# Small transposes as products with the identity, and a scaling moved from GpSimd's keys to VectorE's products, in a chunked recurrence

## The chip, the cores and the metric

The kernel runs on one core of a Trainium2 chip. The metric is the device time of one execution in microseconds (us): 3152.22 us, the median of three runs (3151.61 to 3154.9). Engine names in the profile: PE is TensorE, PEld its weight loads, DVE is VectorE, ACT is ScalarE, POOL is GpSimd, SP is the queue that issues the DMAs. Matrix products here are in float32; PE's clock has two levels, 1.2 and 2.4 GHz, which the profile shows as a granted share of 0.50 and 1.00.

## The reference

Three blocks over 512 latent tokens and 256 context tokens of 1024 channels: two transformer layers, and a third block that mixes a gated short convolution with a recurrence of eight heads, followed by a mixture of 16 experts. The change lies in that recurrence, which runs once forwards and once backwards over the tokens. Per head, with a state S of 64 values x 64 keys:

```python
def step(s, inp):
    r_t, w_t, k_t, v_t, a_t, b_t = inp
    sa = jnp.einsum('bhvk,bhk->bhv', s, a_t)
    s = s * w_t[:, :, None, :] + sa[..., :, None] * b_t[:, :, None, :] + v_t[..., :, None] * k_t[:, :, None, :]
```

The context gives the state in which the latents start.

## The kernel before, in words

The recurrence is computed in chunks of 64 tokens. Both directions are worked on at once: rows 0 to 63 of every tile belong to the forward direction (d = 0), rows 64 to 127 to the backward one (d = 1). `rwkv_prep` builds the operands of all chunks, `rwkv_scan` then walks from chunk to chunk. `rwkv_prep` runs three times, and these are the three stretches of which the prediction speaks:

- the context's, 8 heads and 4 chunks, beside the last feed-forward products of the second layer (lines 430, 432, 435), at about 1860 to 2040 us of the span;
- the first four latent heads', 8 chunks, beside the projections of the third block (the same lines), about 2100 to 2330 us;
- the other four latent heads', beside an output projection (line 2258) and the normalising of the first heads (lines 1174, 1187, 2201, 2215), about 2400 to 2560 us.

Within one `rwkv_prep`, after the elementwise work:

1. `products` (line 1909) multiplies keys and queries; VectorE masks the results into `M1`.
2. `tri_inverse` inverts triangular 64 x 64 blocks: VectorE runs 62 small operations, each of which needs the one before, and then 32 x 32 transposes (lines 2014, 2029, 2037, 2038). Their result feeds PE's 32 x 32 products (lines 2045, 2055).
3. `value_part` runs beside it. For each chunk: a product (1909), ScalarE takes it out of PSUM, GpSimd masks it (`M2`), PE multiplies it with the values (lines 1957, 1967). Then `by_time(kts)` turns the keys: GpSimd scales each head's keys by `pc0`, the decay over the whole chunk, in place (lines 1924 to 1926); PE transposes 64 x 64 blocks, one for each chunk, head and direction, with `flip` (lines 1771 and 1773); 16 of them fill a PSUM bank, which ScalarE empties. Then `kv`: products of the turned keys and the values (line 1981), one bank for each chunk, emptied by ScalarE (line 1983). Then `by_time(bts)` does the same turning for the second set of keys.

`flip` has two forms. The block that goes to rows 0 to 63 of PSUM is a transpose instruction (line 1771), the one that goes to rows 64 to 127 a product with the identity (line 1773). The loop in `by_time` takes d = 0 and d = 1 in turn, so the two forms alternate on PE.

A float32 product is two records in the trace (two weight loads and two matmuls), a transpose one.

`pcs` holds the same decays as `pc0`, but the backward half is ordered by step and not by chunk, as `kv` is; GpSimd copies them (lines 1895, 1897) before the products of step 1.

Generators (`braid`, `weave`) mix a stretch's parts at given rates, and each engine's list of instructions is fixed when the program is built; an engine takes its list strictly in order. PSUM has eight banks of 512 columns, divided between the parts: five for the latents' `rwkv_prep`, three for what runs beside it (in the second latent stretch), and a part waits when all its banks are full. Most elementwise instructions are issued by helpers and carry the helper's line: 382 (`act`, ScalarE), 385 (`tt`, tensor_tensor on VectorE or GpSimd), 388 (`stt`).

Of the kernel before, what the change touches and what calls it, by code (L numbers as in the profile page):

```python
# [167 lines left out]
def _run(g):  # L168
    """a generator to its end -> what it returns"""
    try:  # L170
        while True:
            next(g)
    except StopIteration as e:
        return e.value


def _parts(t):
    """two ranges of tokens"""
    return [(0, TL), (TL, TA)] if t == TA else [(0, TC), (TC, TL)]


class _Hook:
    """a generator step by step; what it returns"""
# [19 lines left out]
class _Arena:  # L203
    """SBUF, float32 left of a movable bound and float32r right of it, each side a stack of tiles.
    Long-lived buffers lie at the outer ends, transient ones rotate near the bound.
    Zones set memory aside for work that other work is to overlap."""
# [37 lines left out]
    def move(self, mid, *cuts):  # L244
        """float32 up to mid floats, float32r behind; new tiles end at the cuts"""
# [18 lines left out]
    def reserve(self, z, n, dt=F32, below=SIZE):  # L264
        """set n floats aside for zone z"""
# [48 lines left out]
    def forget(self, n):  # L314
        """the order of the last releases alone counts from here on"""
# [45 lines left out]
class _K:  # L361
# [50 lines left out]
    def prefetch(self, key, src):  # L412
        """split weights ahead of their use"""
        self.pre[key] = self.wsplit(src, top=True)
# [10 lines left out]
    def gemm(self, w, nk, acts, outs):  # L425
        """outs: list of (psum AP, token slice); w: function (hi|lo, k) -> lhsT; acts: list of (hi, lo) per k"""
# [22 lines left out]
    def rstd_cols(self, cols, n, scale, eps, op=OP.add):  # L449
        """1 / sqrt(cols * scale <op> eps), with a Newton step behind the square root's table"""  # L450
# [11 lines left out]
    def rms_bcast(self, acc, t, nfeat):  # L462
        """acc [128, t]: sums of squares per partition; -> bank with 1/rms on every partition"""
# [9 lines left out]
    def col_bcast(self, r, n):  # L473
        """[128, n] -> bank with the n * 128 values along each partition"""
# [6 lines left out]
    def sumsq(self, blocks, t, w=None, bufs=None, pool=None):  # L481
        """sum over blocks of squares, [128, t]; with w a second one, of the blocks times columns of w"""
# [21 lines left out]
    def modulate(self, xs, t, pb, segs, us=None, dve=()):  # L504
        """xs: list of f32 [128, t]; segs: list of (slice, scale fn(k), shift fn(k)); us: two APs for the normed values or
        None; -> list of (hi, lo) Bufs"""
# [17 lines left out]
    def norm_parts(self, xs, t, nfeat, segs, pool=0, low=((), ())):  # L524
        """normed and modulated blocks, range of tokens by range -> list of (hi, lo) Bufs"""
# [12 lines left out]
    def modulate_part(self, outs, xs, t0, t1, r, segs, low=()):  # L538
        """low: the blocks whose low part is left to GpSimd"""
# [22 lines left out]
    # log1p(e) for 0 <= e <= 1, elementwise on small tiles  # L562
# [31 lines left out]
    def ada(self, parts, w=2):  # L594
        """parameters of layer 0 -> Buf [128, 48, 2]: block-major vectors, (latent, context); params 1 and 4 are 1 + scale"""
# [30 lines left out]
    def ada_first(self, h):  # L626
        """half h of the blocks of layer 0's first shift and scale"""
# [15 lines left out]
        # block 8 j + 4 h + n at column (n, j, v)  # L643
# [8 lines left out]
    def ada_rows(self):  # L652
        """the same for layers 1 and 2 (context: shift and scale 0 alone), as VectorE's sums of products along the rows of
        the transposed weights"""
# [37 lines left out]
    # ---------------------------------------------------------------- layer 0  # L692
# [49 lines left out]
    def gated(self, x, p, P, gate, n, t0, t1, two):  # L742
        """x += gate * p over a range of tokens"""
# [5 lines left out]
    def out_proj(self, w, y, T, x, P, gate, k0=0, name=None, hook=None):  # L749
        """x += gate * (rows k0... of w)^T y; with a hook range of tokens by range, and the hook behind each"""  # L750
# [28 lines left out]
    def step(self, g, n, z=1):  # L779
        """n steps of work in a zone"""  # L780
# [8 lines left out]
    def ffn(self, l, P, T, x, a, side, rate, start=0, hook=None):  # L789
        """x += gate * swiglu(a); a: normed blocks as (hi, lo) Bufs; the last sums range of tokens by range, with a hook  # L790
        behind each"""
# [5 lines left out]
        def outs(bg, bu, bc, t0, t1):  # L797
            """gate's and up's PSUM over a range of tokens"""
# [27 lines left out]
        for g, nb in enumerate(FFG):  # L826
            j0 = 0
            last = g == len(FFG) - 1
            if g == 0:
                # the first two blocks range by range: the second range's norm is under way  # L830
# [55 lines left out]
    def mixer0(self, ab, P):  # L886
# [7 lines left out]
        # dt, [16, tokens]  # L894
# [1846 lines left out]
```

## Time and profile before

| | |
|---|---|
| median of the runs | 3152.22 us |
| profiled execution, first to last instruction (span) | 3154.1 us |
| PE busy | 2976.9 us, 94% |
| DVE busy | 1702.1 us, 54% |
| ACT busy | 989.3 us, 31% |
| POOL busy | 312.5 us, 10% |
| mean granted clock of PE | 0.947 |
| share of PE in the chain that ended last | 71% |
| of it, line 1773 and line 1771 | 2% and 1% of the span |

The profile gives no other time of the profiled execution than its span; it lies inside the range of the three runs. Busy shares are means over stages with different limits, so the stretches are read one by one. "Idle before, releaser" is the time for which an engine stood still before an instruction, and whose work ended that wait. Matmuls are pipelined: a record's duration is longer than the distance to the next record's start, and it is the distance that PE's time is made of.

### The profile page before, as it was taken

What the parts mean: (1) busy time and instruction counts of PE and PEld (TensorE: products, weight loads), DVE (VectorE), ACT (ScalarE), POOL (GpSimd) and SP (SyncE); (2) the same over time, 40 slices, a digit from 0 to 9 for tenths busy, and PEclk for the clock granted to TensorE, in tenths of its full rate; (3) what the DMA queues carried; (4) which work ended last, traced back from release to release, by engine and by line L of the source; (5) the groups of instructions that cost most, each with busy time, mean ns of one, the idle gap of its engine ahead of it and who ended that gap; (6) DMA issues with size and microseconds to landing.
All of it is one profiled execution on the core that took longest, in us unless ns stands there. A gap on an engine that the chain in (4) does not pass through costs nothing.

```text
span 3154.1 us, 43364 instructions
## 1 busy us (share of the span) xinstructions
PE 2976.9 (94%) x17688; PEld 2113.3 (67%) x17688; DVE 1702.1 (54%) x2713; ACT 989.3 (31%) x1625; POOL 312.5 (10%) x287
## 2 busy tenths in 40 slices
PE   7999999999999989999999999988899998999997
PEld 4776558888888877554788777775675565344443
DVE  5865557675764355565755762388636734112113
ACT  5421445412121165333544422244323313000001
POOL 0124310000000010111000000002201311000000
PEclk9999999999999999999999999888888877999999
DMA  6334451474563031001322222131113124999998
GB/s 216 106 103 124 137 175 58 152 257 157 165 226 134 11 125 40 22 22 45 108 95 74 95 79 75 34 108 64 55 38 106 41 85 173 377 409 409 409 409 303
DMA packets 170584, 458.97 MB, mean 146 GB/s; under 512 B 20320, under 2 KB 52704, under 8 KB 170000
## 3 DMA queue, kind: packets, MB, share of 16 engines
q1 hardware_dynamic: 170384, 456.19, 41.0%
q8 instruction: 139, 2.28, 0.3%
q14 instruction: 61, 0.50, 0.0%
HBM read 441.35 MB, written 14.78 MB: 145 GB/s over the span
## 4 chain that ended last, share of the span: by engine, by line
PE 71%; DVE 9%; DMA 5%; issue 3%; ACT 3%; POOL 2%; SPq 0%; DVEq 0%; POOLq 0%; ACTq 0%
PE ps L430 13%; PE ps L432 12%; PE ps L435 12%; PE ps L2598 9%; DVE mem L385 4%; ACT mem L382 3%; PE ps L1614 3%; PE ps L1773 2%; PE ps L2581 2%; DMA mem<-in_wadt_dram 2%; DVE mem L388 1%; POOL mem L385 1%; PE ps L1771 1%; PE ps L606 1%; PE ps L2258 1%
## 5 line engine op out<-in xcount | busy, mean ns | idle before, releaser
L382 ACT ACTIVATE mem<-mem 128x1024 fp32r<-128x1024 f32 (+16 forms) x802 | 543.2, 707 | 850.0 <-PE ps L435 225.3
L385 DVE TENSOR_TENSOR mem<-mem,mem 128x1024 fp32r<-128x1024 f32 (+13 forms) x595 | 515.5, 882 | 394.3 <-ACT mem L382 197.4
L382 ACT ACTIVATE mem<-ps 128x512 f32<-128x512 f32 (+8 forms) x627 | 321.0, 525 | 1130.8 <-PE ps L435 318.4
L430 PE MATMUL ps<-mem,mem 128*128 128x512 f32 (+3 forms) x1991 | 601.4, 359 | 16.1 <-ACT mem L382 13.1
L432 PE MATMUL ps<-mem,mem 128*128 128x512 f32 (+2 forms) x1906 | 569.4, 354 | 1.0 <-DVE mem L385 0.9
L435 PE MATMUL ps<-mem,mem 128*128 128x512 f32 (+2 forms) x1977 | 417.8, 352 | 0.0
L430 PEld LDWEIGHTS ps<-mem,mem 128*128 128x128 f32 (+2 forms) x1991 | 339.9, 189 | 88.0 <-ACT mem L382 19.6
L432 PEld LDWEIGHTS ps<-mem,mem 128*128 128x128 f32 (+1 forms) x1906 | 327.9, 189 | 59.9 <-issue 5.9
L435 PEld LDWEIGHTS ps<-mem,mem 128*128 128x128 f32 (+1 forms) x1977 | 323.7, 189 | 56.2 <-issue 4.1
L2598 PE MATMUL ps<-mem,mem 128*64 128x512 f32 x1344 | 309.2, 598 | 1.0 <-ACT mem L382 0.5
L385 POOL TENSOR_TENSOR mem<-mem 128x256 f32<-128x256 f32 (+4 forms) x84 | 106.1, 1269 | 1810.6 <-ACT mem L382 1411.2
L432 PE MATMUL ps<-mem 128*128 128x512 f32 (+1 forms) x814 | 275.1, 368 | 1.4 <-POOL mem L385 1.0
L430 PE MATMUL ps<-mem 128*128 128x512 f32 (+1 forms) x729 | 258.2, 378 | 10.1 <-ACT mem L382 7.8
L385 DVE TENSOR_TENSOR mem<-mem,ps 128x512 f32<-128x512 f32 (+5 forms) x234 | 128.9, 582 | 236.0 <-PE ps L2598 103.5
L385 DVE TENSOR_TENSOR mem<-mem 128x256 f32<-128x256 f32 (+19 forms) x347 | 186.6, 546 | 85.3 <-ACT mem L382 36.2
L2598 PEld LDWEIGHTS ps<-mem,mem 128*64 128x64 f32 x1344 | 107.1, 137 | 177.9 <-issue 165.7
L385 POOL TENSOR_TENSOR mem<-mem,mem 128x512 f32<-128x512 f32 (+6 forms) x108 | 145.3, 1357 | 515.4 <-ACT mem L382 402.1
L432 PEld LDWEIGHTS ps<-mem 128*128 128x128 f32 x814 | 154.9, 197 | 30.9 <-issue 4.4
L435 PE MATMUL ps<-mem 128*128 128x512 f32 (+3 forms) x743 | 170.7, 359 | 0.0
L430 PEld LDWEIGHTS ps<-mem 128*128 128x128 f32 x729 | 141.5, 199 | 43.5 <-ACT mem L382 12.7
L385 DVE TENSOR_TENSOR mem<-ps,mem 128x512 f32<-128x512 f32 (+6 forms) x176 | 114.2, 664 | 98.3 <-PE ps L1107 37.0
L388 DVE SCALAR_TENSOR_TENSOR mem<-ps,mem 128x256 f32<-128x256 f32 (+1 forms) x232 | 114.8, 534 | 96.8 <-PE ps L435 96.2
(303 smaller groups left out, 3091.0 us busy)
## 6 DMA issues: line engine op xcount, KB each, us to landing
mem<-in_eg_dram SPq DMA_DIRECT2D x128, 512.0 KB, 10.2
mem<-in_eu_dram SPq DMA_DIRECT2D x128, 512.0 KB, 10.2
mem<-in_ed_dram SPq DMA_DIRECT2D x128, 512.0 KB, 10.2
mem<-in_wadt_dram SPq DMA_DIRECT2D x96, 512.0 KB, 4.3
mem<-in_wup_dram SPq DMA_DIRECT2D x44, 512.0 KB, 3.5
mem<-in_wgate_dram SPq DMA_DIRECT2D x44, 512.0 KB, 3.5
mem<-in_wdown_dram SPq DMA_DIRECT2D x40, 512.0 KB, 3.5
mem<-in_w2in_dram SPq DMA_DIRECT2D x35, 512.0 KB, 3.6
```

The lines of the kernel that those rows point to most:

```text
L382: return self.nc.scalar.activation(out, in_, func, **kw)
L385: return (eng or self.nc.vector).tensor_tensor(out, a, b, op=op)
L388: return self.nc.vector.scalar_tensor_tensor(out, a, s, b, op0=op0, op1=op1)
L430: mm(o, w(0, k), acts[k][0][:, ts], start=(k == 0), stop=False)
L432: mm(o, w(0, k), acts[k][1][:, ts], start=False, stop=False)
L435: mm(o, w(1, k), acts[k][0][:, ts], start=False, stop=(k == nk - 1))
L606: nc.tensor.matmul(b.a[32 * q:32 * q + 32, :], cs.a[:, k, :], raw.a[:, j * 512:(j + 1) * 512], start=(k == 0), stop=(k == 7))
L1614: mm(po.a[64 * i:64 * i + 64, :], v.a[:, kb, 64 * h:64 * h + 64], pt.a[:, i, :], start=(kb == 0), stop=(kb == 5))
L1771: self.nc.tensor.transpose(out, src, i)
L1773: self.nc.tensor.matmul(out, src, i, start=True, stop=True)
L2581: mm(b.a[:, :256], ht.a[:, c, fs], o, start=(c == 0), stop=(c == 3))
L2598: mm(bk.a[64 * i:64 * i + 64, 512 * n:512 * n + 512], lhs(k, i), w[i][:, 512 * n:512 * n + 512], start=(k == 0), stop=(k == 7))
```

## The change

All 64 x 64 blocks are turned by a product with the identity; the transpose instruction is gone from `flip`. For the keys `kts`, GpSimd's scaling ahead of the turning is left out; since the decay over a chunk belongs to a key, which is a row of `kv`, the product `kv` is multiplied by it instead, by VectorE on the way out of PSUM, where ScalarE copied before. The keys `bts` are scaled by GpSimd as before. The rest of the diff takes comments out, which moves line numbers: 1773 becomes 1770, 1981 becomes 1978, 1957 becomes 1954, 2037 becomes 2035, 2045 becomes 2043, 2258 becomes 2256.

```diff
     def flip(self, out, src, to, frm):
         i = self.ident.a[64 * frm:64 * frm + 64, 64 * frm:64 * frm + 64]
-        if to == 0:
-            self.nc.tensor.transpose(out, src, i)
-        else:
-            self.nc.tensor.matmul(out, src, i, start=True, stop=True)
+        self.nc.tensor.matmul(out, src, i, start=True, stop=True)
...
-        def by_time(src):
-            for j in range(nh):
+        def by_time(src, scaled):
+            for j in range(nh) if scaled else ():
                 sj = c3(src.a[:, j])
                 self.tt(sj, sj, pc0.a[:, :, j:j + 1].to_broadcast([128, nch, 64]), OP.mult, nc.gpsimd)
...
-            kt = yield from by_time(kts)
+            kt = yield from by_time(kts, False)
...
-                self.act(kv.a[:, i].rearrange("p h v -> p (h v)"), b.a[:, :W])
+                self.tt(kv.a[:, i], b.a[:, :W].rearrange("p (h v) -> p h v", v=64),
+                        pcs.a[:, i].unsqueeze(2).to_broadcast([128, nh, 64]), OP.mult)
...
-            bt = yield from by_time(bts)
+            bt = yield from by_time(bts, True)
```

PE's list in the second latent stretch, where the turning of `kts` ends (L1771 and L1773, L1770 after the change) and the products `kv` begin (L1981, L1978), with the output projection between (L2258, L2256). Before:

```order
L1771 MATMUL ps<-mem_64,mem_13639 64x64
L1773 MATMUL ps<-mem_64,mem_13639 64x64
L2258 MATMUL ps<-mem_15888,mem_15892 128x512 x4
L1981 MATMUL ps<-mem_13639,mem_15888 64x64 x24
L2201 MATMUL ps<-mem_64 64x512 x2
L1981 MATMUL ps<-mem_13639,mem_15888 64x64 x16
L2201 MATMUL ps<-mem_64 64x512
L1174 MATMUL ps<-mem_64,mem_15888 128x2 x4
L2201 MATMUL ps<-mem_64 64x512
L1981 MATMUL ps<-mem_13639,mem_15888 64x64 x16
```

The same place after the change:

```order
L1770 MATMUL ps<-mem_64,mem_13631 64x64 x48
L2256 MATMUL ps<-mem_15876,mem_15880 128x512 x4
L1978 MATMUL ps<-mem_13631,mem_15876 64x64 x24
L2199 MATMUL ps<-mem_64 64x512 x2
L1978 MATMUL ps<-mem_13631,mem_15876 64x64 x16
L2199 MATMUL ps<-mem_64 64x512
L1174 MATMUL ps<-mem_64,mem_15876 128x2 x4
L2199 MATMUL ps<-mem_64 64x512
L1978 MATMUL ps<-mem_13631,mem_15876 64x64 x16
```

The places stay; the 24 alternating pairs, of which the last is shown, become one run of 48 equal products.

POOL's list in the first latent stretch: copies of the decays (L1895 and L1897, later L1892 and L1894), scalings of keys (128x512 from one memory region), masks of `M2` (the rows that also read `mem_64`). Before:

```order
L1895 COPY mem_64<-mem_13639 64x32
L1897 COPY mem_64<-mem_13639 64x4 x8
L385 TENSOR_TENSOR mem_13639<-mem_13639 128x512 x4
L385 TENSOR_TENSOR mem_13639<-mem_13639,mem_64 128x512 x7
L385 TENSOR_TENSOR mem_13639<-mem_13639 128x512 x4
L385 TENSOR_TENSOR mem_13639<-mem_13639,mem_64 128x512
L385 TENSOR_TENSOR mem_64<-mem_64 128x256
```

After:

```order
L1892 COPY mem_64<-mem_13631 64x32
L1894 COPY mem_64<-mem_13631 64x4 x8
L385 TENSOR_TENSOR mem_13631<-mem_13631 128x512 x4
L385 TENSOR_TENSOR mem_13631<-mem_13631,mem_64 128x512 x8
L385 TENSOR_TENSOR mem_64<-mem_64 128x256
```

The four scalings of `kts`, which stood between the seventh mask and the eighth, are gone; those of `bts` stand ahead of the masks, as before.

DVE's list in the second latent stretch, at the end of `tri_inverse` (its last small operations, then its transposes). Before:

```order
L385 TENSOR_TENSOR mem_13639<-mem_13639 128x31 x2
L2037 STREAM_TRANSPOSE mem_13639<-mem_13639 32x1024
L2029 STREAM_TRANSPOSE mem_13639<-mem_13639 32x32x32 x4
L2038 STREAM_TRANSPOSE mem_13639<-mem_13639 32x1024
L2037 STREAM_TRANSPOSE mem_13639<-mem_13639 32x1024
L2038 STREAM_TRANSPOSE mem_13639<-mem_13639 32x1024
L385 TENSOR_TENSOR mem_64<-mem_64 128x256
```

After, with the `kv` rows reading PSUM (`ps`):

```order
L385 TENSOR_TENSOR mem_13631<-mem_13631 128x31 x2
L2035 STREAM_TRANSPOSE mem_13631<-mem_13631 32x1024
L2027 STREAM_TRANSPOSE mem_13631<-mem_13631 32x32x32 x4
L2036 STREAM_TRANSPOSE mem_13631<-mem_13631 32x1024
L2035 STREAM_TRANSPOSE mem_13631<-mem_13631 32x1024
L385 TENSOR_TENSOR mem_13631<-ps,mem_64 128x256
L2036 STREAM_TRANSPOSE mem_13631<-mem_13631 32x1024
L385 TENSOR_TENSOR mem_13631<-ps,mem_64 128x256 x4
L385 TENSOR_TENSOR mem_64<-mem_64 128x256
```

The eight multiplications of `kv` (the last three follow soon behind) stand at the end of VectorE's chain, the first of them behind seven of its eight transposes. In the first latent stretch five of them stand among the last ten of the chain's 31 steps, two in the middle of its transposes, one behind the chain.

## Rows read from the trace of the kernel before

**Rows 1.** Groups by line (count | busy us, mean ns | idle): 1771 in 1945:2060, 2200:2400, 2480:2560.

```profile
L1771 PE MATMUL ps<-mem,mem 64*64 64x64 f32 x64 | 16.6, 259 | 0.0
...
L1771 PE MATMUL ps<-mem,mem 64*64 64x64 f32 x64 | 18.2, 285 | 0.0
...
L1771 PE MATMUL ps<-mem,mem 64*64 64x64 f32 x64 | 19.4, 303 | 0.0
```

**Rows 2.** Timeline of PE, second latent stretch: start, us, what [idle before].

```profile
2494.13 0.24 PE L1771 MATMUL ps<-mem,mem 64*64 64x64 f32 x1
2494.30 0.32 PE L1773 MATMUL ps<-mem,mem 64*64 64x64 f32 x2
2494.56 0.24 PE L1771 MATMUL ps<-mem,mem 64*64 64x64 f32 x1
...
2497.13 0.31 PE L1771 MATMUL ps<-mem,mem 64*64 64x64 f32 x1
2497.38 0.47 PE L1773 MATMUL ps<-mem,mem 64*64 64x64 f32 x2
2497.78 0.31 PE L1771 MATMUL ps<-mem,mem 64*64 64x64 f32 x1
```

**Rows 3.** Timeline of PE, same stretch: products of the same shape.

```profile
2482.04 1.12 PE L1957 MATMUL ps<-mem,mem 64*64 64x64 f32 x16 [2.64 <-POOL mem L385]
2482.94 1.06 PE L1967 MATMUL ps<-mem,mem 64*64 64x64 f32 x16
...
2515.56 1.15 PE L1981 MATMUL ps<-mem,mem 64*64 64x64 f32 x32
2516.64 1.07 PE L2201 MATMUL ps<-mem 128*64 128x512 f32 x2
...
2519.63 1.15 PE L1981 MATMUL ps<-mem,mem 64*64 64x64 f32 x32
```

**Rows 4.** Windows: length, busy of PE, PEld, DVE, ACT, POOL, granted clock, DMA.

```profile
1951.00:1954.40 3.40, 3.40 (x10) 2.68 (x10) 0.01 (x1) 1.65 (x2) 0.00 (x0) 0.50 0.08 34
2259.00:2265.00 6.00, 6.00 (x16) 4.69 (x15) 0.00 (x0) 0.60 (x1) 0.00 (x0) 0.50 0.00 0
2482.00:2489.00 7.00, 6.96 (x56) 5.05 (x56) 6.52 (x15) 1.14 (x3) 1.18 (x1) 0.50 0.22 75
2494.10:2497.10 3.00, 3.00 (x22) 2.06 (x21) 2.87 (x5) 0.69 (x1) 1.26 (x1) 1.00 0.42 113
2511.00:2524.40 13.40, 13.40 (x221) 9.19 (x219) 1.86 (x7) 7.06 (x15) 1.95 (x2) 1.00 0.25 81
2524.50:2561.90 37.40, 37.40 (x321) 26.65 (x319) 3.83 (x6) 7.95 (x15) 0.00 (x0) 0.50 0.13 43
```

**Rows 5.** Timeline of POOL and PE, first latent stretch: scalings, last mask, its reader.

```profile
2232.78 6.15 POOL L385 TENSOR_TENSOR mem<-mem 128x512 f32<-128x512 f32 x4 [1.51 <-PE ps L1909]
2238.90 1.39 POOL L385 TENSOR_TENSOR mem<-mem,mem 128x512 f32<-128x512 f32 x1
...
2240.34 1.12 PE L1957 MATMUL ps<-mem,mem 64*64 64x64 f32 x16 [4.96 <-POOL mem L385]
```

**Rows 6.** Waits of DVE in 2240:2290: us in total, times, longest.

```profile
DVE mem L385 <- PE ps L435: 21.9, 3, 13.3
```

**Rows 7.** Timeline of DVE and PE: where PE meets `tri_inverse`, first and second stretch.

```profile
2290.38 1.19 PE L2045 MATMUL ps<-mem,mem 32*32 32x32 f32 x32 [2.02 <-DVE mem L2029]
...
2505.49 1.24 DVE L2037 STREAM_TRANSPOSE mem<-mem 32x1024 f32<-32x1024 f32 x1
2506.76 1.24 DVE L2038 STREAM_TRANSPOSE mem<-mem 32x1024 f32<-32x1024 f32 x1
```

**Rows 8.** Groups of DVE by form: 2474.6:2483.4 (POOL works), then 2483.6:2494.6 (POOL idle).

```profile
L385 DVE TENSOR_TENSOR mem<-mem 128x252 f32<-128x252 f32 x2 | 2.5, 1260 | 0.1
...
L385 DVE TENSOR_TENSOR mem<-mem 128x252 f32<-128x252 f32 x2 | 0.8, 422 | 0.1
```

**Rows 9.** Groups of DVE by form, 2330:2390: the scan's products leaving PSUM.

```profile
L385 DVE TENSOR_TENSOR mem<-ps,mem 128x256 f32<-128x256 f32 x15 | 6.4, 424 | 13.6 <-PE ps L2104 13.4
```

## The prediction

> **What bounds the kernel now.** I read the page first: PE is busy for 94% of the span and makes 71% of the chain of waits, so I looked for places where PE's own instructions get shorter, and where PE waits. The groups by line show the turning of the keys as two lines: 192 transposes (line 1771) and 192 products of two records each (line 1773), and PE stands idle before none of the transposes [rows 1]. The timeline of PE shows what they cost. Between two transposes lie 2494.56 - 2494.13 = 0.43 us in one place and 2497.78 - 2497.13 = 0.65 us in another, each time for one transpose and one product [rows 2]; the durations of the transposes, 0.24 and 0.31 us, tell the two places apart, and they are PE's two clock levels: the first lies in a window granted 1.00, and flips at 2482 to 2489 and from 2524.5 on stand in windows granted 0.50 [rows 4].
>
> The same timeline shows products of the same shape, 64 x 64 float32 on alternating halves, without transposes between them: 32 records in 2516.64 - 2515.56 = 1.08 us, 34 ns each; and at the lower clock 16 records in 2482.94 - 2482.04 = 0.90 us, 56 ns each [rows 3, 4]. So two products, four records, take 0.135 us at 2.4 GHz and 0.225 us at 1.2 GHz, where the pair of a transpose and a product takes 0.43 and 0.65. The reader is to see that the product of line 1773 takes 0.26 us behind a transpose (2494.30 to 2494.56) and that line 1981's takes 0.067 behind another product: most of the pair's time lies in the change from one kind to the other.
>
> Three places matter beside that. PE waits for GpSimd's masks, 4.96 us in the first latent stretch, behind four scalings that take 6.15 us [rows 5], and 2.64 us in the second [rows 3]. VectorE's operations take 1.26 us instead of 0.42 while GpSimd works [rows 8]. And VectorE's inversion meets PE at line 2045, where PE already waits 2.02 us for it in the first latent stretch [rows 7].
>
> **The change part by part.** *The flips.* The mean of a transpose's duration gives the share at the lower clock: (259 - 240) / 70 = 27%, then 64% and 90% in the three stretches [rows 1, 2]. A pair takes 0.43 + 0.22 x share = 0.49, 0.57 and 0.63 us; 64 pairs each make 31, 37 and 40 us, 108 in all. After the change 64 pairs take 8.6 us at the high and 14.4 at the low clock. If all of it were on the path the gain would be 108 - 26 = 82 or 108 - 43 = 65 us, and what decides is what is late next in each stretch.
>
> *Context.* No flip waits for anything here [rows 1], and in the window shown VectorE is busy for 0.01 and ScalarE for 1.65 of 3.40 us [rows 4], so nothing else becomes late soon: 31 - 8.6 = 22.7, less 2 because some pairs are interrupted by large products whose time I counted with theirs. The clock falls behind flips here: ten large products take 3.40 us at 0.50 [rows 4], one of four such places with 13 us together; half of that, 6.5, is what a clock that stays up gives back, nothing is the other end, and I take 4, nearer the upper end since line 1981's products run at 1.00 [rows 3, 4]. Sum 25.
>
> *First latent stretch.* Without the scalings the last mask starts when ScalarE has copied its input, some 5 us earlier, so the wait of 4.96 goes [rows 5]. Up to the meeting at line 2045 stand 32 pairs: 32 x (0.57 - 0.18) = 12.5, with 0.18 as the middle of the two prices. Large products at 0.50 for 6.00 us [rows 4] return 3 at most. PE's side: 20.5. VectorE's side: it waits 21.9 us for PE's line 435 in this stretch, and these waits shrink as PE comes earlier [rows 6]; four scalings less make its chain 4 x 0.84 = 3.4 faster [rows 8], five multiplications of kv ahead of the meeting make it 5 x 0.42 = 2.1 slower [rows 9]; at most 23. Both sides agree on about 20; PE is already the one that waits, so I take 19. Behind the meeting are 32 pairs more, mostly at 0.50: 32 x (0.62 - 0.225) = 12.6, of which the first eight pairs' 3 us are lost, because the second group of 32 x 32 products waits for the end of VectorE's chain; 10 are left. Sum 29.
>
> *Second latent stretch.* PE's side up to kv: 2.64 [rows 3] and 32 x (0.63 - 0.18) = 14.4, 17 us and more. But here VectorE decides. Its chain does not wait for PE; the first multiplication of kv stands behind its seventh transpose, which ends at 2505.49 + 1.24 = 2506.7 [rows 7], less 3.4 for the four scalings: 2503.3. Five banks hold five products kv; the sixth needs the bank that this multiplication empties, so PE passes its third group of kv at 2503.3 + 0.4 = 2503.7 instead of 2519.63 [rows 3]. That is a new wait of PE of 3 to 10 us. What is queued behind it on PE is the 32 x 32 products of line 2045, which need the chain's last transpose anyway, and the last flips. With one more transpose (1.24) for the seventh product, the flips that began at 2524.5, with the last window of [rows 4], begin 14.7 us earlier. Behind them 32 pairs at 0.50: 32 x (0.65 - 0.225) = 13.6. I cost the ScalarE copies between lines 2045 and 2055 at 1.5 us: eight pairs covered them, now it is five. Sum 26.8.
>
> *kv on VectorE instead of ScalarE.* VectorE's nearest row is 0.42 us for 128 x 256 out of PSUM [rows 9]; 16 of these and four of twice the size are about 10 us of VectorE. In the context VectorE has room, in the other two it is counted above. From below: nothing, if they all stand in its waits; from above: 10.
>
> Total 25 + 29 + 27 = 81 us. The profiled execution's span is 3154.1, so 3073; it lies 1.9 us above the median of the runs, 3152.2, so 3071 by that. I say 3072.
>
> **The rivals.** *The clock stays up (3051).* The clock is 0.50 for 37.40 us where the last flips of the second latent stretch stand [rows 4]. If flips alone pull it down, these too run at 1.00: 32 pairs at 0.135 instead of 0.225 in both latent stretches give 6, the 17 us of other products in that window give 8, the like in the first stretch 4, the context 2.5: 20 more, a gain of 101. The Trainium skill says in "TensorE: Matmul & The Clock Gate", Part 4 (PE-mode transpose), that transposes do not count as a busy PE for the clock gate; by it the clock would be back in all three stretches. Against that, the clock falls at 2524.5 behind 13.40 us without a single flip, granted 1.00, whose last part are 32 x 32 products [rows 3, 4], so I think those pull it down too, and they stay.
>
> *VectorE's chain decides everywhere (3097).* Its waits for PE may turn out not to shorten, for instance because the kv multiplications stand ahead of its last steps in the first stretch and make it wait for PE in turn. Then the meetings come earlier only by the masks and by GpSimd's absence: 8 instead of 19, and 8 instead of 14.7. With the clock in the context unpaid (4) and half of the flips there at the lower clock's price (4, of the 5.8 between 14.4 and 8.6), the gain is 81 - 11 - 7 - 4 - 4 = 55. For it: VectorE is busy without a gap in the second stretch. Against it: 21.9 us of waits for PE in the first [rows 6].
>
> *The turning is dearer (3168).* Suppose the 0.26 us of line 1773's product at the high clock and 0.40 at the low one (2497.38 to 2497.78) are its own price and not that of the change from one kind to the other. Then 192 transposes of 0.17 and 0.25 us become products of 0.26 and 0.40: 192 x (0.4 x 0.09 + 0.6 x 0.15) = 24 us more [rows 2], less the 8 us of masks: 16 slower. It decides from the point where a product behind a product costs more than the transpose, 0.17. The Trainium skill asks in "Perfetto Trace Analysis", section Transposes, that a logical transpose be a transpose and not a standard matmul; by it the change is a loss. Against that, lines 1957 and 1981 have the same shape and the same alternation of halves, and take 0.067 to 0.112 [rows 3].
>
> *It does little (3130).* The saved time is taken up at once by some wait that I don't see, and only masks, part of the context and a few flips remain: 22. Against it stands that PE has no idle time before the flips.
>
> **How the numbers follow.** The forecast, a gain of 65 to 95, has 56%; the clock 15%; VectorE's chain 20%; little 5%; slower 4%. A measurement of this kernel tells about 0.2%, 6 us, from no change. So faster 94%, no change 2%, slower 4%. The range runs from a gain of 106, the clock's case, to one of 47, the chain's with the lower clock throughout: 3046 to 3105.
>
> **What would show it.** Right: line 1770 with 768 records, in runs of 34 ns each where the clock is 1.00; no wait of line 1954 behind four scalings; the context's stretch some 25 us shorter with the clock at 1.00 between 1940 and 1975; PE waiting for VectorE at line 1978's third group and at line 2043. Wrong: records of line 1770 more than 60 ns apart, which would be the dear turning; PE's idle time before lines 2043 and 1978 above 15 us in a stretch, which would be VectorE's chain; or granted 1.00 through the last flips, which would make me too careful.

## The result, and the profile after

The changed kernel takes 3067.47 us, the median of four runs (3062.72 to 3073.18), against 3153.56 us of the kernel before on the same chip (four runs, 3151.61 to 3155.82): a ratio of 0.973, 95% interval 0.9716 to 0.9747. The forecast was 3072, with a range of 3046 to 3105. The profiled execution took 3062.72 us, the fastest of the four, and its span is 3061.0; between the two profiled spans lie 93.1 us, more than the 86 between the medians. Of these, 4.0 stand already ahead of the first instruction that the change touches (1934.04 before, 1930.00 after, first rows below), so 89 come from the stretches of the change and what lies between them.

The windows of the three stretches, before and then after: the columns are window, length, then busy us of PE, its weight loads, DVE, ACT and POOL with their records, granted clock, DMA share and GB/s. The context's window runs from its last products with the values to the last product of its scan, the first latent one from the first product of line 1909 (1906 after) to its last of the scan, the second one up to the experts' first gather.

```profile
1934.04:2063.47 129.43, 126.82 (x1008) 98.67 (x1006) 45.88 (x80) 33.65 (x57) 7.84 (x7) 0.88 0.13 42
2160.36:2382.11 221.75, 196.77 (x2015) 149.20 (x2014) 133.00 (x211) 59.09 (x106) 43.26 (x39) 0.82 0.14 45
2425.67:2659.49 233.82, 210.84 (x2062) 138.41 (x2061) 139.12 (x265) 68.14 (x142) 58.20 (x60) 0.79 0.29 96
```

```profile
1930.00:2028.50 98.50, 96.02 (x1063) 79.00 (x1062) 46.33 (x76) 30.43 (x51) 7.81 (x7) 1.00 0.17 55
2129.48:2313.50 184.02, 163.40 (x2079) 129.86 (x2078) 132.30 (x219) 55.96 (x98) 37.80 (x35) 0.90 0.17 55
2357.07:2565.78 208.71, 177.96 (x2126) 121.80 (x2125) 141.94 (x273) 65.67 (x134) 52.84 (x56) 0.85 0.32 108
```

PE's idle time is length less busy time. The flips' time is the sum, over their records, of the distance to PE's next record. What is left of a stretch's gain is other work of PE that ran faster, and the last column but two of the rows shows why: the granted clock rose in each. The records' starts bear this out: of PE's time in other work 19.3, 41.6 and 51.9 us stood at 0.50 before and 0, 23.1 and 41.2 after, and half of what went is 9.7, 9.3 and 5.4 us.

| stretch | shorter by | flips, before to after | PE idle, before to after | rest: other work, faster |
|---|---|---|---|---|
| context | 30.9 | 31.2 to 9.4: 21.8 | 2.6 to 2.5: 0.1 | 9.0 |
| first latent | 37.7 | 35.8 to 11.0: 24.8 | 25.0 to 20.6: 4.4 | 8.5 |
| second latent | 25.1 | 39.5 to 11.0: 28.5 | 23.0 to 30.8: -7.8 | 4.4 |

Between context and first latent stretch 4.1 us were given back, where no changed line stands (96.9 us before, 101.0 after, granted 0.91 and 0.90). The table compares one profile of each kernel, and further down two profiles of one kernel differ by up to 6 us in a latent stretch, so its smaller numbers may be scatter.

The flips themselves, from PE's timeline after (start, us, what, [idle before]); they answer to [rows 2], in the context and in the first latent stretch behind 32 x 32 products:

```profile
1949.61 1.15 PE L1770 MATMUL ps<-mem,mem 64*64 64x64 f32 x32
1950.69 0.50 PE L430 MATMUL ps<-mem,mem 128*128 128x512 f32 x1
...
2257.31 4.26 PE L1770 MATMUL ps<-mem,mem 64*64 64x64 f32 x76
2261.50 0.50 PE L430 MATMUL ps<-mem 128*128 128x512 f32 x1
```

At the high clock 32 records, eight pairs, take 1950.69 - 1949.61 = 1.08 us, 0.135 us a pair instead of 0.43; behind line 2053 the 76 records take 4.19 us, 55 ns each, the price of the low clock (granted 0.50 from 2254.55 to 2261.38).

The place of [rows 3] in the second latent stretch, and after it VectorE's list at the same time:

```profile
2427.41 1.07 PE L2199 MATMUL ps<-mem 128*64 128x512 f32 x2
2438.27 1.12 PE L1978 MATMUL ps<-mem,mem 64*64 64x64 f32 x16 [9.79 <-DVE mem L385]
2440.00 1.12 PE L1978 MATMUL ps<-mem,mem 64*64 64x64 f32 x16 [0.61 <-DVE mem L385]
2441.05 0.31 PE L2043 MATMUL ps<-mem 32*32 32x32 f32 x2
```

```profile
2436.53 1.24 DVE L2035 STREAM_TRANSPOSE mem<-mem 32x1024 f32<-32x1024 f32 x1
2437.80 0.42 DVE L385 TENSOR_TENSOR mem<-ps,mem 128x256 f32<-128x256 f32 x1
2438.25 1.24 DVE L2036 STREAM_TRANSPOSE mem<-mem 32x1024 f32<-32x1024 f32 x1
2439.53 1.42 DVE L385 TENSOR_TENSOR mem<-ps,mem 128x256 f32<-128x256 f32 x4
```

PE stands still for 9.79 us until VectorE has passed its seventh transpose and done the first multiplication of kv, 0.42 us, which empties the bank that PE needs. It is the new wait that the prediction described. The clock falls while PE waits there, in this window after:

```profile
2432.05:2455.94 23.89, 17.05 (x232) 14.80 (x233) 13.43 (x23) 4.32 (x8) 0.73 (x1) 0.50 0.01 1
```

What stands behind the wait pays for that. These are the 32 x 32 products and the first of the last flips, before and then after:

```profile
2521.86 2.04 PE L2045 MATMUL ps<-mem 32*32 32x32 f32 x62
2524.45 0.31 PE L1771 MATMUL ps<-mem,mem 64*64 64x64 f32 x1
```

```profile
2443.09 3.33 PE L2043 MATMUL ps<-mem 32*32 32x32 f32 x62
2447.25 1.49 PE L1770 MATMUL ps<-mem,mem 64*64 64x64 f32 x24
```

### The profile page after: what moved, and what is told of

It reads as the page before. It is cut to its first block, busy times and chain, and to the rows that moved or that the text cites. A ratio compares the mean times of both kernels' runs of the same rounds, so it can differ in the third digit from the quotient of the medians.

```text
span 3061.0 us, 43732 instructions
## 1 busy us (share of the span) xinstructions
PE 2879.1 (94%) x17880; PEld 2056.7 (67%) x17880; DVE 1703.4 (56%) x2733; ACT 982.3 (32%) x1605; POOL 297.6 (10%) x271
## 4 chain that ended last, share of the span: by engine, by line
PE 69%; DVE 10%; DMA 5%; issue 4%; ACT 3%; POOL 1%; SPq 0%; DVEq 0%; ACTq 0%; POOLq 0%
PE ps L430 13%; PE ps L432 13%; PE ps L435 13%; PE ps L2596 9%; DVE mem L385 5%; ACT mem L382 3%; PE ps L1614 3%; PE ps L2579 2%; DVE mem L388 1%; DMA mem<-in_wadt_dram 1%; PE ps L606 1%; PE ps L1607 1%; PE ps L1770 1%; PE ps L1583 1%; POOL mem L385 1%
## 5 line engine op out<-in xcount | busy, mean ns | idle before, releaser
L385 DVE TENSOR_TENSOR mem<-mem,mem 128x1024 fp32r<-128x1024 f32 (+13 forms) x595 | 508.5, 871 | 380.6 <-ACT mem L382 188.0
L382 ACT ACTIVATE mem<-ps 128x512 f32<-128x512 f32 (+8 forms) x607 | 313.1, 529 | 1026.5 <-PE ps L435 327.1
L432 PE MATMUL ps<-mem 128*128 128x512 f32 (+1 forms) x814 | 272.2, 364 | 1.3 <-POOL mem L385 0.9
L430 PE MATMUL ps<-mem 128*128 128x512 f32 (+1 forms) x729 | 254.4, 373 | 11.8 <-ACT mem L382 7.9
L385 POOL TENSOR_TENSOR mem<-mem 128x256 f32<-128x256 f32 (+4 forms) x72 | 96.1, 1336 | 1706.5 <-ACT mem L382 1382.7
L385 DVE TENSOR_TENSOR mem<-ps,mem 128x512 f32<-128x512 f32 (+6 forms) x196 | 123.0, 643 | 99.4 <-PE ps L1107 35.4
```

Source lines behind the costliest of these rows:

```text
L382: return self.nc.scalar.activation(out, in_, func, **kw)
L385: return (eng or self.nc.vector).tensor_tensor(out, a, b, op=op)
L430: mm(o, w(0, k), acts[k][0][:, ts], start=(k == 0), stop=False)
L432: mm(o, w(0, k), acts[k][1][:, ts], start=False, stop=False)
```

## The experiments

Ratios are to the kernel before on the same chip, with 95% intervals. Flips alone, the scaling alone, kinds grouped and flips twice shared one chip; halves grouped, kv by VectorE and the first runs of the two versions without either scaling another; the four side by side a third. In a diff, `...` stands for what is left out.

**Which half of the change counts.** *Flips alone:* in the kernel before, `flip` as in the kernel after.

```diff
-        if to == 0:
-            self.nc.tensor.transpose(out, src, i)
-        else:
-            self.nc.tensor.matmul(out, src, i, start=True, stop=True)
+        self.nc.tensor.matmul(out, src, i, start=True, stop=True)
```

> The kernel before, with all 64 x 64 blocks turned by products and nothing else; GpSimd still scales the keys, ScalarE still copies kv. Theory (PE's own time at the flips is the gain): the flips fall from 106.5 us of PE (sum over the trace of before) to about 31, of which some 70 us reach the end, 3083 us; PE's wait of 5 us for GpSimd's last mask in the first latent stretch and of 2.6 us in the second stay. Rival (GpSimd's scalings and their contention with VectorE are the larger half, and flips alone are eaten by waits for the masks and for VectorE's chain): a gain of 40 us or less, 3113 us or more, with PE waits of over 10 us for POOL or DVE in the latent stretches.

Measured: 3067.35 us, 0.9729 (0.9708 to 0.9751): the whole gain of the change, 16 us better than expected. The waits for the masks stay, and there is none at the products kv:

```profile
PE ps L1954 <- POOL mem L385: 6.7, 4, 2.6
...
PE ps L2042 <- DVE mem L2034: 1.6, 1, 1.6
```

(Waits of PE in the second latent stretch: us in total, times, longest.)

*The scaling alone:* the kernel after, with the old `flip`.

> The kernel after, with flip in its two old forms again, so that only the scaling is moved from GpSimd's keys to VectorE's products. Theory: the masks' waits go (5 us and 2.6 us); PE is so late at kv and at line 2043 that VectorE's work there hides; a gain of 8 to 12 us, 3143 us, and no PE wait at line 1978 for VectorE. Rival (the scalings are the larger half): a gain of 40 us or more, 3113 us or less. Other rival (VectorE's added multiplications cost what GpSimd's absence gives): within 3 us of before.

Measured: 3141.33 us, 0.9955 (0.9939 to 0.997): a gain of 14 us, a little above the theory's 8 to 12. In its profile, which is that of the slowest of ten runs, the first latent stretch is 9.8 us shorter than before, the second 7.2, and the context 1.3 longer with its clock still down:

```profile
1939.61:2070.36 130.75, 128.13 (x1008) 99.56 (x1006) 48.08 (x83) 31.31 (x53) 7.85 (x7) 0.87 0.13 41
```

So the halves don't add: 88 and 14 by themselves, 86 together. That the scaling's 14 us are to be had only while the flips make PE late is my reading of this; the wait at kv, taken up below, is the part of it that a trace shows.

**Why a pair took 0.43 us.** *Kinds grouped:* the kernel before, with the same instructions in another order.

```diff
-                for c in range(c0, c0 + cb):
+                for d, c in [(d, c) for d in range(2) for c in range(c0, c0 + cb)]:
                     for j in range(nh):
-                        for d in range(2):
...
```

> The kernel before, with only the order in a bank changed: the eight transposes first, then the eight products, so that a bank has one change from transposes to products and one back instead of eight of each. No instruction is added or taken out. Theory (the change from one kind to the other is dear, 0.10 us one way and 0.19 us the other): a transpose behind a transpose takes no more than a product behind a product, 0.07 us at the high clock; a bank of eight pairs takes 1.1 to 1.4 us instead of 3.4; gain 50 to 65 us, some 3095 us. Rival (a transpose is dear wherever it stands, 0.17 us at the high clock and 0.25 at the low one): transposes 0.17 us apart, a bank 1.9 us or more, gain 25 to 35 us, some 3123 us. Second rival (the alternation of halves, not of kinds, made before quick, and two of one half in a row are slower): no gain or a loss.

Measured: 3076.48 us, 0.9763 (0.9732 to 0.9794). One bank in its timeline of PE:

```profile
1956.92 0.63 PE L1771 MATMUL ps<-mem,mem 64*64 64x64 f32 x8
1957.48 1.14 PE L1773 MATMUL ps<-mem,mem 64*64 64x64 f32 x16
1958.56 0.50 PE L430 MATMUL ps<-mem,mem 128*128 128x512 f32 x1
```

A transpose behind a transpose takes 0.56 / 8 = 0.070 us, as the theory said and far below the rival's 0.17. The products take 1.08 / 8 = 0.135 us each, though, twice what a product of alternating halves takes, so the bank takes 1.64 us and not 1.1 to 1.4. The pair's own price is 0.205 us; of the 0.43 the change from one kind to the other and back made 0.225. These averages still hold one change at each end of a run. By the starts of the single records the transposes inside the run stand 56 ns apart (146 at the last) and the records of the products 58 to 59 ns (106 at the first, 148 at the last), so that the change makes 0.43 - 0.056 - 0.117 = 0.25 us. A run of line 1770 in the kernel after ends with the same 148 ns before a large product, with no transpose near, so a price of this size comes with other changes of shape as well. The gain is 79 us from the order alone, 59 of it at the flips (106.5 to 47.3), and more than either expectation, since the context's clock came back here as well, with all transposes still in it:

```profile
1932.67:2035.72 103.05, 100.44 (x1008) 83.31 (x1006) 45.86 (x80) 33.73 (x57) 7.86 (x7) 1.00 0.16 52
```

*Halves grouped:* the kernel after with the same new order of loops.

> The kernel after, with only the order in a bank changed: eight products of the forward half, then eight of the backward half, instead of alternating. In the run with kinds grouped, products of one half stood 67 ns per record, twice the 34 ns of alternating halves. Theory (products of the two halves overlap on PE only when they alternate): 67 ns per record at the high clock throughout, 50 to 57 us of PE for the 768 records instead of 31, which is the dose of the run with flips issued twice; so 14 to 20 us slower than after, some 3084 us. Rival (the 67 ns there came from the transposes nearby): 34 ns per record, within 4 us of after, 3067 us.

Measured: 3081.31 us, 0.9785 (0.9756 to 0.9814). A bank:

```profile
1950.58 1.90 PE L1770 MATMUL ps<-mem,mem 64*64 64x64 f32 x32
1952.41 0.50 PE L430 MATMUL ps<-mem,mem 128*128 128x512 f32 x1
```

32 records take 1.83 us, 57 ns each instead of 34 (somewhat less than the 67 expected, which held the ends of a shorter run), 51.1 us over all flips instead of 31.4. The theory holds, and the starts of the single records show how: where the halves alternate, a record of each half starts within 6 or 7 ns and the next two 58 to 59 ns after the first; in a run of one half a single record stands 58 to 59 ns behind the one before it. In the run with flips twice, below, two products of one half follow each other, and the records still start in such twos.

**What a microsecond of flips is worth.** *Flips twice:* the kernel after, each product issued a second time into the same place.

```diff
-                            self.flip(b.a[half(d), col:col + 64], ...)
+                            for _ in range(2):
+                                self.flip(b.a[half(d), col:col + 64], ...)
```

> The kernel after with each flip issued twice (the second product writes the same block again): 384 products, 768 records more. Theory (PE decides except where it waits for VectorE): 31 us more of PE, of which the second latent stretch hides 4.4 us ahead of line 1978 and the first some 2 ahead of line 2043: 25 us slower than after, 3092 us. Rival (VectorE's chain decides at both meetings, so that flips ahead of them are free): 16 us slower, 3083 us. Other rival (longer runs of small products pull the clock down in the context, too): 35 us or more slower, 3102 us.

Measured: 3083.1 us, 0.9775 (0.9748 to 0.9801), 16 us slower than after (14 by the ratios, since after was timed on another chip), as the rival said. The flips took 56.7 us, 25.3 more. In the context 7.8 us more of flips made the stretch 7.9 longer, in the first latent 8.5 made it 10.1 longer, in the second 8.9 made it 4.8 longer, and the wait at kv fell from 10.4 to 5.4:

```profile
PE ps L1979 <- DVE mem L385: 5.4, 1, 5.4
```

So PE decides in the context and, as far as one profile tells, in the first latent stretch, and shares with VectorE in the second; the rival's number came out, not its reason. The context's clock stayed at 1.00, against the other rival.

**What the wait at kv costs.** *kv by VectorE:* flips alone, but VectorE copies kv out of PSUM.

```diff
-                self.act(kv.a[:, i].rearrange("p h v -> p (h v)"), b.a[:, :W])
+                nc.vector.tensor_copy(kv.a[:, i].rearrange("p h v -> p (h v)"), b.a[:, :W])
```

> The kernel before with all flips as products and GpSimd's scalings kept, as in the run with flips alone, but kv leaves PSUM by a copy on VectorE instead of ScalarE (no scaling moved). Theory (VectorE's work on kv, which stands in its list between the last steps of the chain, holds PE at the products kv of the second latent stretch): 6 to 10 us slower than flips alone, 3076 us, with a PE wait of 8 us or more for VectorE at the products kv. Rival (that wait in the kernel after costs nothing, since PE would wait for the chain at the next line anyway): within 3 us of flips alone, 3067 us.

Measured: 3066.41 us, 0.973 (0.9708 to 0.9753). The wait came, 5.9 us in all, 5.3 the longest and not 8 or more, and the time is that of flips alone: my theory falls by its own measure. The second latent stretch is indeed 8.2 us longer than in the first profile of flips alone (212.2 against 204.0, or 206.7 in the second profile), the first 4.4 us shorter (182.8 against 187.2), so what this wait costs the whole stays open.

**Versions without either scaling.** *Scaling in the scan:* kv leaves by ScalarE as before, and the decay is applied where the scan uses kv.

```diff
...
-                    self.tt(u.a, S, pcs.a[:, i, :]..., OP.mult, nc.gpsimd)
-                    self.tt(u.a, u.a, kv.a[:, i], OP.add, nc.gpsimd)
+                    self.tt(u.a, S, kv.a[:, i], OP.add, nc.gpsimd)
+                    self.tt(u.a, u.a, pcs.a[:, i, :]..., OP.mult, nc.gpsimd)
...
```

> The kernel after, but ScalarE copies kv as before the change and the scaling is folded into the scan, where GpSimd computes (S + kv) * pcs in the two operations in which it computed S * pcs + kv; one multiplication on VectorE is added for the context's first chunk. So neither GpSimd's scaling of the keys nor VectorE's multiplications of kv are left. Theory (in the kernel after, the masks' waits that went were paid for by the wait at kv): both gains together, 8 to 10 us faster than after, 3058 us, with PE waiting under 3 us at the products kv. Rival (VectorE's chain decides the second latent stretch however kv leaves PSUM): 1 to 3 us faster, 3065 us. Other rival (two more or later ScalarE copies ahead of the 32 x 32 products cost as much): no change.

Measured: 3061.38 us, 0.9711 (0.9689 to 0.9733), 6 us ahead of after and not 8 to 10. *Both in the scan:* GpSimd's scaling of the second keys goes too, and VectorE multiplies the new state by the decay.

> As the version with the scaling in the scan, but the second keys are left unscaled as well: GpSimd computes S + kv, VectorE adds the product and then multiplies the sum with pcs, one more VectorE operation of 0.42 us per chunk in the scan (18 in all, on the scan's chain); GpSimd's scalings are all gone. Theory (contention with GpSimd lengthens VectorE's chain by up to 3.4 us in each latent stretch, and the scan's chain takes the 18 x 0.42 = 7.6 us back in part, since other products run beside it in the latents): within 4 us of the version with one scaling folded, 3058 us. Rival (the scan's chain is bare): 6 to 8 us slower than that version. Rival (GpSimd's scalings were the larger cost): 5 us or more faster than it.

Measured: 3058.36 us, 0.9696 (0.9673 to 0.9718), 3 us ahead of the version with one scaling in the scan, as the theory said. Of PE's waits in the second latent stretch, 10.4 us at kv in the kernel after, the first of these versions keeps half, 3.1 and 2.2, at the next meeting with VectorE's chain:

```profile
PE ps L2042 <- DVE mem L2034: 3.1, 1, 3.1
PE ps L1954 <- POOL mem L385: 3.1, 4, 2.0
...
PE ps L2042 <- DVE mem L2026: 2.2, 1, 2.2
```

**The four side by side.** Since these times lie within 10 us, the kernel after, flips alone and both versions were run again on one chip.

> The kernel after, once more, beside the three below on one chip, because the differences between these four (0 to 10 us) are as large as the spread of the runs of one of them. Theory: 3067 us, and in the second latent stretch PE waits 5 to 10 us for VectorE at the products kv, so that this stretch (from the first product of line 1906 to the first of the experts' gathers) gets 21 to 26 us shorter than before. Rival (the wait in the first profile was a chance of that run): no such wait, the stretch 30 us or more shorter.

> The kernel before with only the flips as products, once more. Theory (the move of the scaling gives some us by the masks in both latent stretches and loses as many at kv in the second): within 3 us of after, second latent stretch 29 to 34 us shorter than before, first 34 to 36. Rival (the scaling's move is worth its 14 us here, too): 10 us or more slower than after.

> The version with the scaling of kv in the scan, once more. Theory: 4 to 8 us faster than after on the same chip, 3061 us; no PE wait at the products kv, the second latent stretch 33 us shorter than before. Rival: the same as after within 3 us, its better median so far being chance.

> The version with both scalings in the scan, once more. Theory (no scaling on GpSimd before the inversion's end, so VectorE's chain is the shortest of all): 6 to 12 us faster than after, 3058 us; the second latent stretch gives back some 5 us in its scan, where VectorE has one more operation per chunk. Rival: the same as the version with one scaling folded within 2 us.

| | median (range) us | ratio, 95% interval | first latent | second latent |
|---|---|---|---|---|
| after | 3063.68 (3058.68 to 3072.96) | 0.9724, 0.9700 to 0.9749 | 37.7, 40.7 | 25.1, 25.7 |
| flips alone | 3067.39 (3060.01 to 3069.57) | 0.9727, 0.9702 to 0.9752 | 34.5, 29.6 | 29.8, 27.1 |
| scaling in the scan | 3061.02 (3054.93 to 3064.87) | 0.9707, 0.9682 to 0.9732 | 36.7, 30.9 | 33.7, 28.4 |
| both in the scan | 3057.96 (3054.51 to 3063.71) | 0.9703, 0.9678 to 0.9728 | 41.0, 38.5 | 30.4, 25.6 |

The last columns are the us by which the stretches are shorter than before, in the first and the second profile of each kernel; there is one profile of the kernel before. The expectation for after held. The others were partly missed: flips alone came 3.7 us behind after instead of within 3 and gained less in both stretches than the 34 to 36 and 29 to 34 expected, the scaling in the scan is 2.7 us ahead of after and not 4 to 8, and both in the scan 5.7, just below 6 to 12. The wait at kv was 10.4 us in both profiles of the kernel after. One kernel's stretch differs by up to 6 us between two profiles, and the granted clock goes with it; the first latent stretch of flips alone:

```profile
2137.90:2325.11 187.21, 163.00 (x2078) 129.39 (x2078) 133.74 (x211) 58.86 (x106) 41.42 (x39) 0.91 0.17 54
```

```profile
2128.71:2320.83 192.12, 164.76 (x2078) 130.32 (x2078) 132.93 (x211) 58.70 (x106) 43.73 (x39) 0.88 0.16 52
```

What follows: in the two pairs of profiles the first latent stretch of after is 3 and 11 us shorter and the second 5 and 1 longer than those of flips alone, differences no larger, but for the 11, than those between two profiles of one kernel, and no difference of the whole can be told. Both scalings in the scan had the best median both times, 6 us ahead of the kernel after on one chip, but the ranges overlap; it is likely the better version, not shown to be.

## Why the prediction was right, point by point

*The flips.* Predicted 31, 37 and 40 us, measured 31.2, 35.8 and 39.5; after the change 9.4, 11.0 and 11.0, between the two prices used. This step carried the result, and the reason given for it, that most of the pair's time lies in the change from one kind to the other, was shown by the run with kinds grouped: 0.225 of 0.43 us by the averages of a bank, 0.25 by the records inside the runs. What it left out is the other part: 0.07 us more (0.06 inside the runs) go because products of alternating halves start side by side. The rival of the dearer turning is out. The Trainium skill's rule behind that rival ("Perfetto Trace Analysis", Transposes) agrees with a transpose by itself, 0.070 us against 0.135 for a product of one half, and not with 64 x 64 blocks on alternating halves, where a product takes 0.067. A page of the Trainium skill that I had not weighed fits the trace better: "TensorEngine Tiling (Array Packing)" says under Key Properties that a change of tiling mode drains the engine and that different tiles work in parallel, and under Restrictions that column tiling excludes transpose mode for float32. By it each transpose would be a change of mode there and back; the runs agree in the 0.225 us, in the 34 against 57 ns, and in the 148 ns that also end a run of products alone, but no record shows the mode.

*Context, 25.* Measured 30.9. The flips' 20.7 came as 21.8; the clock's term, 4 with 6.5 as its end, was mis-sized: 9.0. I counted four places of large products at 0.50; the granted 0.88 over 129.43 us means 31 us at half speed, flips and shorter products among them, and all of it went. The 4.1 us given back behind the context were not foreseen; with flips alone it was 8.5 in one profile and 4.1 in the other, so part of it may be scatter.

*First latent stretch, 29.* Measured 37.7: 22.7 up to the meeting at line 2045, where 19 were forecast, and 15.0 behind it instead of 10. Flips, counted as 22.1 with the eight pairs lost, gave 24.8; the clock, at most 3, gave 8.5. PE's idle time fell by 4.4, most of it at the place of [rows 5], where PE waited 4.96 us for the mask (3.75 with flips alone) and after the change waits 0.80:

```profile
2204.85 0.68 PE L1954 MATMUL ps<-mem,mem 64*64 64x64 f32 x16 [0.80 <-POOL mem L385]
```

Both sides had been put at about 20 up to the meeting, and both came that much earlier: VectorE's waits for line 435 fell from 21.9 us [rows 6] to 1.2, and PE still waits for VectorE at the meeting, 1.8 us instead of 2.02 [rows 7].

*Second latent stretch, 26.8.* Measured 25.1, but as the sum of two errors that cancel, and that is luck. The last flips were to begin 14.7 us earlier and began 8.6 earlier (2447.25 - 2357.07 = 90.2 us behind the stretch's first product instead of 2524.45 - 2425.67 = 98.8). Behind them 12.1 were forecast and 16.5 measured.

VectorE decided, as said, at the place said: the wait was put at 3 to 10 us and took 10.4. But PE was to pass its third group of kv 15.9 us earlier and passed it 12.8 earlier (81.2 us behind the stretch's first product instead of 94.0). One term of this was mis-sized, the 3.4 us by which VectorE's chain was to be faster without the four scalings. The chain from its first transposes to the last four is shown here for the kernel before, for after, and for flips alone, where GpSimd still scales:

```profile
2452.64 8.23 DVE L2014 STREAM_TRANSPOSE mem<-mem 32x1024 f32<-32x1024 f32 x4
...
2495.99 8.23 DVE L2029 STREAM_TRANSPOSE mem<-mem 32x1024 f32<-32x1024 f32 x4
```

```profile
2384.95 8.21 DVE L2012 STREAM_TRANSPOSE mem<-mem 32x1024 f32<-32x1024 f32 x4
...
2427.03 8.21 DVE L2027 STREAM_TRANSPOSE mem<-mem 32x1024 f32<-32x1024 f32 x4
```

```profile
2396.49 8.16 DVE L2011 STREAM_TRANSPOSE mem<-mem 32x1024 f32<-32x1024 f32 x4
...
2441.23 8.40 DVE L2026 STREAM_TRANSPOSE mem<-mem 32x1024 f32<-32x1024 f32 x4
```

It takes 43.4, 42.1 and 44.7 us. Against before, which the prediction started from, the chain is 1.3 us faster and not 3.4 (0.9 by the second profile of after, 42.4); against flips alone it is 2.7 (2.0 in the second pair of profiles, 42.4 and 44.4). Why the same scalings cost more beside the faster flips isn't shown.

The other part had no term at all: PE's clock falls in the new wait. From the third group to the last flips PE needed 9.0 us instead of 4.8 (0.6 of it another wait), at 0.50 where before it was 1.00 [rows 4]. With flips alone, where no such wait stands, the clock fell later, at 2452.36, and the same piece took 7.6 us, 1.6 of them a wait for the chain. Behind the flips it is the other way round: the clock was at 0.50 for 37.4 us there before [rows 4], and after the change from 2447.25 to 2455.94 and for 6.8 us more (2459.35 to 2466.18).

*The rival of the clock, 15%.* Half of it happened: the clock stayed at 1.00 through the context, and in the latents it still fell, at 32 x 32 products as forecast and in the wait at kv. Its reason is not shown: by the Trainium skill ("TensorE: Matmul & The Clock Gate", Part 4) transposes don't count as a busy PE in the same way, but the run with kinds grouped has every transpose of the kernel before and 1.00 in the context. Since the transposes take less of PE's time in that run, it doesn't refute the rule. What goes with the low clock there is the alternation (0.88 before, 0.87 with the scaling alone).

*What was wrong inside the right sum.* The masks' waits, the four scalings and their contention were counted as a gain to the end, some 5 us in the first latent stretch, and the second one's cost was taken as a limit and not as a loss. Flips alone reached the same time without them. In the second stretch a trace shows where the gain goes. Flips alone begin the products kv and pass their third group, without a wait, here:

```profile
2440.64 1.61 PE L1978 MATMUL ps<-mem,mem 64*64 64x64 f32 x48
...
2447.26 1.15 PE L1978 MATMUL ps<-mem,mem 64*64 64x64 f32 x32
```

That is 74.6 and 81.2 us behind the first product of the stretch. The kernel after begins them 9.9 us sooner, at 64.7, then waits, and passes the third group at 81.2 as well (in the second profiles 71.6 and 78.2 with flips alone, 63.9 and 80.4 after). What PE had gained up to kv is given back there. Between the two latent stretches flips alone are another 2.6 us shorter than after, in both pairs of profiles; why isn't shown.

The sum came out near, 81 against 86 in the medians, although the clock's terms, 7 in all, were some 15 too small. Against that stand the second stretch's shortfall ahead of its last flips, the 4.1 us given back behind the context, and a profile that is the fastest of four runs. To that extent the nearness is luck.

## What to carry to other kernels

Where two kinds of PE instruction alternate, price the pair by the distance between records, not by either duration, and look in the same trace for a run of one kind: the difference is what the order alone can give. Small products that use different halves of PE should alternate between the halves; grouping them cost this kernel 14 us by the medians. Two gains that remove the same lateness don't add, so each part of a change is worth a run of its own. And a new wait should be priced with the clock that PE may lose in it, for what stands behind the wait.

## What the runs showed of the hardware

Of one shape, 64 x 64 in float32 at the high clock, averaged over a run with its ends: a transpose among transposes 0.070 us, a product among products of its own half 0.114 to 0.135, among alternating halves 0.067, and a pair of a transpose and a product in turn 0.43. Inside the runs the first three are 0.056, 0.117 and 0.058. Reordering the same instructions was worth 79 us of 3155.79.

The clock's share of this gain was larger than the prediction's main sum had it: of the 93.7 us by which the three stretches got shorter, 21.9 are other work of PE at a higher granted clock. In the second latent stretch the clock fell to 0.50 during PE's wait of 9.79 us and stayed there until 2455.94, through the 32 x 32 products behind the wait.
